# A ring of weight parts: two places of 1024 columns become four of 512, made and given back by halves

## The chip, the cores and the metric

The kernel runs on one core of a Trainium2 chip. The metric is the device time of one launch in microseconds. A core has TensorE (matrix products; PE in the rows, its weight loads PEld), VectorE (DVE), ScalarE (ACT), GpSimd (POOL) and SyncE (SP, whose queue issues most of the transfers here). Each engine works through its own instructions in order and meets the others at semaphores.

## What is computed

Two model blocks over one sequence of 512 tokens of width 1024, all in float32. The first block mixes tokens in three ways (RWKV-7, S5, gated linear attention), merges them by gates, adds a cross attention to 256 memory tokens and a feed-forward layer with a short convolution. The second has an attention layer with a context of 256 tokens, an HGRN2 layer and a gated feed-forward layer after each. Nearly all of the arithmetic is in products of the tokens with weight matrices:

```
p_rw, p_s5, p_gla, p_gate = _split(h @ w_in[l], IN_SIZES)
gates = jax.nn.sigmoid(p_gate).reshape(B, L, N_BRANCH, D_MODEL)
merged = (gates[:, :, 0] * (y_rw @ w_branch[l, 0])
          + gates[:, :, 1] * (y_s5 @ w_branch[l, 1])
          + gates[:, :, 2] * (y_gla @ w_branch[l, 2]))
x = x + merged @ w_out[l]
x = x + cross_attention(rms_norm(x, norm_xattn[l]), mem_n, xa_wq[l], xa_wkv[l], xa_wo[l])
x = x + conv_ffn(rms_norm(x, norm_ffn[l]), ffn_w_up[l], ffn_conv[l], ffn_conv_b[l], ffn_w_down[l])
```

## The kernel before

Activations lie with features on the 128 partitions and tokens along the columns. To keep float32 accuracy at the matrix engine's faster rate, both operands of a product are split into a high part (a cast to float32r) and a low part (the value less its high part), and three products are summed: low weight by high token, high by low, high by high. The activations' parts (`hh`, `hl`, `mh`, `ml` and others) are made once; the weights' parts are made each time that a weight passes.

A weight, in this text, is what one call of `Stream.weights` (L194) handles: up to eight rows of 128x128 (`ks` rows, 1024 columns in all), or four rows of 256 columns for products whose result has the tokens on the partitions (`tokens`, L245). It passes through two rings. `raw` has three places of 1024 columns, which SyncE's queue fills from HBM (`load`, L189). `parts` has two places of 1024 columns for the high part and two for the low one (`Stream(b, 3, 2)`, L2230). ScalarE casts the whole weight into `wh` (L200), VectorE subtracts the whole into `wl` (L204). In some passages (`st.help` set) the rows are halved for the subtraction alone: VectorE takes the first half, GpSimd the second. Then `multiply` (L233) runs the rows in order on TensorE, three products for each row and each set of tokens (L240; L262 to L264 where weights are the moving operand, L1195 for gates made ahead). When the last of them is done, the place is free for the weight after next.

Most weights have eight rows. Those of `w_branch` and `w_glu` have four and use half a place. The last third of each feed-forward layer's second matrix has six rows, `hg_wo` is taken in calls of four and three rows and one call for its last rows (`last`, L2203). `first_products` (L1230) makes four weights at once in a pool of its own ("first").

Two things set the order of the work. The program is written with fillers: generators whose steps (products, for example) are dropped into chains of small dependent operations. And a scheduler of the framework then lists each engine's instructions by its own model of their times and by the order in the program, waiting for free places of the rings among them. So a change in the rings also moves instructions that it doesn't name. `closing` (L272) is the passage at the end of a layer: the last products run for one half of the tokens, then for the other, while the first half's norm runs beside them; `st.help` is set in it.

The places that the prediction names: the S5 layer (its chain on VectorE through L1052 to L1120, with the scan L1115) has the merge of the first mixer beside it (`merge`, L1203: a gate's weight of eight rows, then a branch's weight of four, then a step on VectorE, L1218, and for later mixers the gate read back from HBM, `th`); `conv_ffn` (L1318) is the first block's feed-forward layer, with the context's norm (`Context.steps`) as its filler.

Of the kernel before, what the change touches and what calls it, by code (L numbers as in the profile page):

```python
# [9 lines left out]
F32 = mybir.dt.float32  # L10
F32R = mybir.dt.float32r
# [6 lines left out]
P = 128  # L18
# [157 lines left out]
class Stream:  # L176
# [16 lines left out]

    def weights(self, src, ks, m=P, parts=None):  # L194

        nc = self.b.nc
        raw = self.load(src, ks, m)
        h, l = ((parts or self.parts).tile([P, 1024], F32R, tag=n, name="w" + n)[:, : ks * m]
                .rearrange("p (k m) -> p k m", m=m) for n in "hl")
        nc.scalar.copy(h, raw)  # L200
        c = ks - ks // 2 if self.help else ks
        for e, s in ((nc.vector, slice(0, c)), (nc.gpsimd, slice(c, ks))):
            if s.stop > s.start:
                e.tensor_tensor(l[:, s], raw[:, s], h[:, s].bitcast(F32), op=ALU.subtract)  # L204
        return h, l

    def accumulators(self, kinds):

# [23 lines left out]

    def multiply(self, parts, ks, sets):  # L233
        nc = self.b.nc
        h, l = parts
        for k in range(ks):
            s = sets(k)
            for w, x, n in ((l, 1, 0), (h, 2, 1), (h, 1, 2)):
                for z in s:
                    nc.tensor.matmul(z[0], w[:, k], z[x], start=k == 0 and n == 0, stop=k == ks - 1 and n == 2)  # L240

    def features(self, *a, **kw):
        for _ in self.products(*a, **kw):
# [2 lines left out]
    def tokens(self, W, ks, xs, ts, gs, take):  # L246


        nc = self.b.nc
        for i, g in enumerate(gs):  # L250
            parts = []
            for q in range(ks // 4):
                h, l = self.weights(W[g, q], 4, 256)
                parts += [(h[:, k], l[:, k]) for k in range(4)]
            for two in [[t] for t in ts[:-2]] + [ts[-2:]]:
                accs = [self.accumulator()[:, :256] for _ in two]
                for q in range(0, ks, 4):
                    for acc, t in zip(accs, two):
                        for k in range(q, q + 4):
                            xh, xl = (z[:, t * P : (t + 1) * P] for z in xs(k))  # L260
                            wh, wl = parts[k]
                            nc.tensor.matmul(acc, xh, wl, start=k == 0, stop=False)  # L262
                            nc.tensor.matmul(acc, xl, wh, start=False, stop=False)  # L263
                            nc.tensor.matmul(acc, xh, wh, start=False, stop=k == ks - 1)  # L264
                for acc, t in zip(accs, two):
                    take(i, t, acc)
                    yield
# [915 lines left out]
def gates(b, st, xs, ns, made, wk, ps):  # L1183


    nc = b.nc
    dram = b.pool("gates", 1, DRAM)
    for n in ns:
        for m in range(8):
            acc = ps.tile([P, 512], F32, tag="ps", name="gate")  # L1190
            h, l = st.weights(b.a["w_gate"][8 * n + m], 8)
            for k in range(8):
                xh, xl = xs(k)
                for w, x, i in ((l, xh, 0), (h, xl, 1), (h, xh, 2)):
                    nc.tensor.matmul(acc, w[:, k], x, start=k + i == 0, stop=k == 7 and i == 2)  # L1195
                if k < 7:
                    yield
            th = wk.tile([P, 512], F32, name="gate", tag="gate")
            nc.scalar.activation(th, acc, AF.Tanh, scale=0.5)
            made[n, m] = dram.tile([P, 512], F32, name=f"gate{n}{m}")  # L1200
            nc.scalar.dma_start(made[n, m], th)
            yield
# [26 lines left out]
def first_products(b, st, W, tiles, h, units, accs, late, side):  # L1229


    hh, hl = h
    with ExitStack() as c:
        pool = b.pool("first", len(tiles), ctx=c, side=side)
        st.help = True
        parts = {m: st.weights(W[m], 8, parts=pool) for m in tiles}
        st.help = False
        for n, (at, to) in enumerate(units):
            for i, m in enumerate(tiles):
                st.multiply(parts[m], 8, lambda k: [(accs[n][m][:, to], hh[:, k, at], hl[:, k, at])])  # L1240
                if n == 0 and i == 1:
                    late()
# [848 lines left out]
def block2(b, st, X, h, late, old_, c, out, ctx):  # L2091
# [86 lines left out]
    with ExitStack() as c1:  # L2178
# [25 lines left out]
        def products(p):  # L2204

            for i in range(8):
                acc = st.accumulator()[:, :256]
                st.multiply([z[:, i : i + 1] for z in last], 1, lambda k: [(acc, *(z[:, p.t] for z in o[7]))])
                add_gated(b, p.X, m.gt1)(i, acc)
                yield  # L2210

# [14 lines left out]
def body(tc, a, out):  # L2226
    with ExitStack() as ctx:
        b = Builder(tc, ctx, a)
        b.common()
        st = Stream(b, 3, 2)  # L2230
        mod = [b.cp.tile([P, 48, 2], F32, name=f"mod{l}") for l in range(2)]
        context = Context(b, ctx, mod)
        c = ctx.enter_context(ExitStack())
        block2(b, st, *block1(b, st, ctx, c, context), context, c, out, ctx)
# [16 lines left out]
```

## Time and profile before

| | us |
|---|---|
| median of three runs | 3227.83 |
| lowest and highest of them | 3222.96, 3229.99 |
| the profiled execution | 3222.53 |
| its span, from first to last instruction | 3220.2 |
| TensorE busy in the span | 3089.4 |
| VectorE, ScalarE, GpSimd busy | 1800.2, 1171.2, 781.7 |
| mean granted clock of TensorE | 0.98 of full speed |

How to read it: the engines work side by side, so the busy times don't add up; a matmul counts as busy up to a modelled end, and the next one starts before that end. The granted clock is the share of TensorE's full speed in a stretch.

### The profile page before, as it was taken

Reading aid. Unit: us, or ns where it says so; the run is one execution under the profiler, and the core shown is the slowest. Engines: PE = TensorE matmul, PEld = TensorE weight load, DVE = VectorE, ACT = ScalarE, POOL = GpSimd, SP = SyncE. Lnnn points to the kernel's source line nnn. Section 1 sums busy time; section 2 is a strip of 40 time slices with the busy share of each in tenths; the row PEclk is TensorE's granted clock in tenths of the full one; section 3 lists DMA queues with packets and bytes.
Section 4 is the critical chain, followed back from the end, with each engine's and each line's share of the span. In section 5 each row is a group of like instructions: output and inputs, shape, how many; then the busy total and the mean of one; then the engine's idle time right before and its main releaser. Section 6 shows DMA issues by size and latency. Waiting matters only on the chain.

```text
span 3220.2 us, 50507 instructions
## 1 busy us (share of the span) xinstructions
PE 3089.4 (96%) x20456; PEld 2644.9 (82%) x20456; DVE 1800.2 (56%) x3067; ACT 1171.2 (36%) x2009; POOL 781.7 (24%) x827
## 2 busy tenths in 40 slices
PE   7999889989999999999999999999999999899998
PEld 6888767769797878896669988888889998788887
DVE  6444475556565555777766684323555555753434
ACT  4233224324344333545654321212444444332223
POOL 3322131220040000568775000000323222310003
PEclk9999989999999999999999999999999999989999
DMA  3122123333245232432224473222321111123333
GB/s 132 57 73 80 38 75 97 98 117 124 78 133 188 89 95 89 134 107 72 80 84 144 146 243 129 61 64 62 109 91 53 53 51 49 53 76 95 98 98 112
DMA packets 114776, 308.11 MB, mean 96 GB/s; under 512 B 32224, under 2 KB 37040, under 8 KB 114032
## 3 DMA queue, kind: packets, MB, share of 16 engines
q1 hardware_dynamic: 109904, 293.94, 29.1%
q10 hardware_dynamic: 4640, 10.95, 0.9%
q8 instruction: 161, 2.64, 0.3%
q14 instruction: 71, 0.58, 0.1%
HBM read 295.18 MB, written 8.39 MB: 94 GB/s over the span
## 4 chain that ended last, share of the span: by engine, by line
PE 84%; DVE 7%; issue 2%; POOL 2%; DMA 2%; ACT 2%; DVEq 0%; POOLq 0%; SPq 0%; ACTq 0%
PE acc L240 57%; PE ps L524 3%; PE gate L1195 3%; PE acc L262 2%; DVE wl L204 2%; PE acc L263 2%; PE acc L264 2%; PE ps L1980 2%; PE mods L1490 1%; PE ss L346 1%; PE sc L1745 1%; PE st L1766 1%; DMA w<-in_ada_dram 1%; DVE y L435 1%; PE acc L1788 1%
## 5 line engine op out<-in xcount | busy, mean ns | idle before, releaser
L240 PE MATMUL acc<-hh,wl 128*128 128x512 f32 (+1 forms) x2296 | 762.3, 364 | 12.3 <-DVE wl L204 7.0
L240 PE MATMUL acc<-hh,wh 128*128 128x512 f32 (+1 forms) x2296 | 759.7, 362 | 0.0
L240 PE MATMUL acc<-hl,wh 128*128 128x512 f32 (+1 forms) x2296 | 758.6, 362 | 0.0
L200 ACT CAST wh<-raw 128x1024 fp32r<-128x1024 f32 (+3 forms) x472 | 460.2, 977 | 580.6 <-PE acc L240 427.0
L204 DVE TENSOR_TENSOR wl<-raw,wh 128x1024 fp32r<-128x1024 f32 (+2 forms) x472 | 527.4, 1118 | 221.5 <-ACT wh L200 214.3
L204 POOL TENSOR_TENSOR wl<-raw,wh 128x512 fp32r<-128x512 f32 (+1 forms) x120 | 169.2, 1413 | 1299.6 <-ACT wh L200 756.1
L240 PEld LDWEIGHTS acc<-hh,wl 128*128 128x128 f32 x2296 | 403.1, 189 | 88.9 <-DVE wl L204 9.4
L240 PEld LDWEIGHTS acc<-hh,wh 128*128 128x128 f32 x2296 | 403.0, 189 | 68.7 <-issue 1.8
L240 PEld LDWEIGHTS acc<-hl,wh 128*128 128x128 f32 x2296 | 402.6, 189 | 65.3 <-issue 0.5
L240 PE MATMUL acc<-mh,wl 128*128 128x512 f32 (+1 forms) x848 | 266.5, 340 | 14.3 <-DVE wl L204 14.1
L240 PE MATMUL acc<-ml,wh 128*128 128x512 f32 (+1 forms) x848 | 261.4, 333 | 0.2 <-DVE ml L340 0.2
L240 PE MATMUL acc<-mh,wh 128*128 128x512 f32 (+1 forms) x848 | 261.3, 333 | 0.0
L240 PEld LDWEIGHTS acc<-mh,wl 128*128 128x128 f32 x848 | 151.6, 189 | 36.1 <-DVE wl L204 18.3
L240 PEld LDWEIGHTS acc<-ml,wh 128*128 128x128 f32 x848 | 152.1, 189 | 17.5 <-DVE ml L340 0.4
L240 PEld LDWEIGHTS acc<-mh,wh 128*128 128x128 f32 x848 | 151.8, 189 | 17.4
L1604 ACT ACTIVATE t<-acc 128x512 f32<-128x512 f32 x66 | 34.7, 527 | 343.6 <-PE acc L240 343.5
L1556 DVE SCALAR_TENSOR_TENSOR X<-acc,mod,X 128x256 f32<-128x256 f32 (+1 forms) x112 | 65.4, 593 | 160.6 <-PE acc L240 160.6
L1605 DVE SCALAR_TENSOR_TENSOR t<-t,acc 128x512 f32<-128x512 f32 x66 | 39.4, 596 | 161.9 <-ACT t L1604 161.9
L262 PE MATMUL acc<-wl,hh 128*128 128x256 f32 x448 | 126.8, 285 | 1.8 <-DVE wl L204 1.0
L263 PE MATMUL acc<-wh,hl 128*128 128x256 f32 x448 | 127.0, 284 | 0.0
L264 PE MATMUL acc<-wh,hh 128*128 128x256 f32 x448 | 126.9, 285 | 0.0
L1606 DVE TENSOR_TENSOR t<-t,acc 128x512 f32<-128x512 f32 x66 | 39.4, 598 | 137.6 <-PE acc L240 137.1
(604 smaller groups left out, 5823.3 us busy)
## 6 DMA issues: line engine op xcount, KB each, us to landing
raw<-in_ffn_in_dram SPq DMA_DIRECT2D x88, 512.0 KB, 3.5
ada<-in_ada_dram SPq DMA_DIRECT2D x48, 512.0 KB, 3.9
w<-in_ada_dram SPq DMA_DIRECT2D x48, 512.0 KB, 4.5
raw<-in_ffn_w_up_dram SPq DMA_DIRECT2D x44, 512.0 KB, 3.5
raw<-in_ffn_out_dram SPq DMA_DIRECT2D x32, 512.0 KB, 3.5
raw<-in_hg_w_dram SPq DMA_DIRECT2D x32, 512.0 KB, 3.5
raw<-in_ffn_out_dram SPq DMA_DIRECT2D x40, 384.0 KB, 3.1
raw<-in_w_gate_dram SPq DMA_DIRECT2D x24, 512.0 KB, 3.6
```

The lines of the kernel that those rows point to most:

```text
L200: nc.scalar.copy(h, raw)
L204: e.tensor_tensor(l[:, s], raw[:, s], h[:, s].bitcast(F32), op=ALU.subtract)
L240: nc.tensor.matmul(z[0], w[:, k], z[x], start=k == 0 and n == 0, stop=k == ks - 1 and n == 2)
L262: nc.tensor.matmul(acc, xh, wl, start=k == 0, stop=False)
L263: nc.tensor.matmul(acc, xl, wh, start=False, stop=False)
L264: nc.tensor.matmul(acc, xh, wh, start=False, stop=k == ks - 1)
L524: nc.tensor.matmul(out(r, ci), lhsT(r, ci), rhs(r, ci), start=start, stop=stop)
L1195: nc.tensor.matmul(acc, w[:, k], x, start=k + i == 0, stop=k == 7 and i == 2)
L1556: return lambda i, acc: b.nc.vector.scalar_tensor_tensor(X[:, i], acc, gate[:, i : i + 1], X[:, i], op0=ALU.mult, op1=ALU.add)
L1605: nc.vector.scalar_tensor_tensor(t, t, 1.0, a, op0=ALU.add, op1=ALU.mult)
L1606: nc.vector.tensor_tensor(t, t, u, op=ALU.mult)
L1980: nc.tensor.matmul(p[:, c], kc[:, c * P : (c + 1) * P], qc[:, c * P : (c + 1) * P], start=True, stop=True)
```

## The change

`weights` makes parts of 512 columns. A weight of eight rows now takes two places in each ring of parts, one after the other: cast of the first four rows, subtraction, cast of the last four rows, subtraction. Four rows of 256 columns are cut into two times two rows. Where `st.help` is set, VectorE subtracts the first part and GpSimd the later one, so that six rows are now divided into four and two where they were three and three, and a weight of four rows of 128 is no longer divided. It returns a list of pairs of rows, and `multiply`, `tokens` and `gates` take the row's pair from it. The rings have four places of 512 columns instead of two of 1024 (`Stream(b, 3, 4)`), the pool "first" twice as many places of half the size: the memory is the same. `raw` and its transfers are as before.

```diff
     def weights(self, src, ks, m=P, parts=None):
 
+
         nc = self.b.nc
         raw = self.load(src, ks, m)
-        h, l = ((parts or self.parts).tile([P, 1024], F32R, tag=n, name="w" + n)[:, : ks * m]
-                .rearrange("p (k m) -> p k m", m=m) for n in "hl")
-        nc.scalar.copy(h, raw)
-        c = ks - ks // 2 if self.help else ks
-        for e, s in ((nc.vector, slice(0, c)), (nc.gpsimd, slice(c, ks))):
-            if s.stop > s.start:
-                e.tensor_tensor(l[:, s], raw[:, s], h[:, s].bitcast(F32), op=ALU.subtract)
-        return h, l
+        out = []
+        step = 512 // m
+        for n, k0 in enumerate(range(0, ks, step)):
+            c = min(step, ks - k0)
+            h, l = ((parts or self.parts).tile([P, 512], F32R, tag=t, name="w" + t)[:, : c * m]
+                    .rearrange("p (k m) -> p k m", m=m) for t in "hl")
+            x = raw[:, k0 : k0 + c]
+            nc.scalar.copy(h, x)
+            (nc.gpsimd if self.help and n else nc.vector).tensor_tensor(l, x, h.bitcast(F32), op=ALU.subtract)
+            out += [(h[:, k], l[:, k]) for k in range(c)]
+        return out
...
     def multiply(self, parts, ks, sets):
         nc = self.b.nc
-        h, l = parts
         for k in range(ks):
+            h, l = parts[k]
             s = sets(k)
             for w, x, n in ((l, 1, 0), (h, 2, 1), (h, 1, 2)):
                 for z in s:
-                    nc.tensor.matmul(z[0], w[:, k], z[x], start=k == 0 and n == 0, stop=k == ks - 1 and n == 2)
+                    nc.tensor.matmul(z[0], w, z[x], start=k == 0 and n == 0, stop=k == ks - 1 and n == 2)
...
             for q in range(ks // 4):
-                h, l = self.weights(W[g, q], 4, 256)
-                parts += [(h[:, k], l[:, k]) for k in range(4)]
+                parts += self.weights(W[g, q], 4, 256)
...
-        pool = b.pool("first", len(tiles), ctx=c, side=side)
+        pool = b.pool("first", 2 * len(tiles), ctx=c, side=side)
...
-                st.multiply([z[:, i : i + 1] for z in last], 1, lambda k: [(acc, *(z[:, p.t] for z in o[7]))])
+                st.multiply(last[i : i + 1], 1, lambda k: [(acc, *(z[:, p.t] for z in o[7]))])
...
-        st = Stream(b, 3, 2)
+        st = Stream(b, 3, 4)
```

`gates` is changed in the same way as `multiply`. The new lines move the line numbers: L200, L204, L1115, L1118, L1218 and L435 of the program before are L206, L207, L1118, L1121, L1222 and L438 of the changed one.

VectorE's order where the merge begins beside S5 (`ysl` is the low part of the first mixer's result, `M` the first merge step, `cs` and `tmp` belong to S5). Before, and then of the change:

```order
L1091 COPY m_4651<-mag_526 128x8x63
L340 SCALAR_TENSOR_TENSOR ysl<-Y_185,ysh 128x512 x3
L1218 SCALAR_TENSOR_TENSOR M<-th,acc 128x512
L204 TENSOR_TENSOR wl<-raw,wh 128x512
L1086 TENSOR_TENSOR tmp<-cs,ph 128x16
L1087 TENSOR_TENSOR tmp<-cs,ph 128x16
L204 TENSOR_TENSOR wl<-raw,wh 128x1024
```

```order
L1094 COPY m_4791<-mag_550 128x8x63
L343 SCALAR_TENSOR_TENSOR ysl<-Y_185,ysh 128x512 x3
L207 TENSOR_TENSOR wl<-raw,wh 128x512
L1222 SCALAR_TENSOR_TENSOR M<-th,acc 128x512
L207 TENSOR_TENSOR wl<-raw,wh 128x512 x2
L1089 TENSOR_TENSOR tmp<-cs,ph 128x16
```

Before, the first merge step, which waits for TensorE's sum, stood ahead of the next branch weight's subtraction of 512; now a subtraction of 512 stands ahead of that step, and two follow it.

VectorE's order further on in S5, from the scan (L1115, now L1118) to the next merge step (`E`, `R`, `sx`, `tmp` belong to S5). Before, and then of the change:

```order
L1115 SCALAR_TENSOR_TENSOR R<-m_4651,z 128x512
L1054 TENSOR_TENSOR E<-E,tmp 128x1024
L1091 COPY m_5138<-mag_526 128x8x63
L1065 TENSOR_TENSOR tmp<-pw,s5c 128x1152
L1118 TENSOR_TENSOR R<-R,cs 128x512
L204 TENSOR_TENSOR wl<-raw,wh 128x1024
L1218 SCALAR_TENSOR_TENSOR M<-th,acc 128x512
```

```order
L1118 SCALAR_TENSOR_TENSOR R<-m_4791,z 128x512
L207 TENSOR_TENSOR wl<-raw,wh 128x512
L1094 COPY m_5294<-mag_550 128x8x63
L1055 TENSOR_TENSOR E<-pw,bb 128x1024
L1121 TENSOR_TENSOR R<-R,cs 128x512
L1057 TENSOR_TENSOR E<-E,tmp 128x1024
L207 TENSOR_TENSOR wl<-raw,wh 128x512
L1123 TENSOR_TENSOR sx<-R,sw 128x8x64
L1068 TENSOR_TENSOR tmp<-pw,s5c 128x1152
L1222 SCALAR_TENSOR_TENSOR M<-th,acc 128x512
L207 TENSOR_TENSOR wl<-raw,wh 128x512 x2
```

The subtraction of 1024 stood behind the scan and four more S5 instructions; now one of 512 stands directly behind the scan, a second four instructions later, and two more behind the merge step.

VectorE's order at the end of the first block's feed-forward layer (`u`, `t` and `ml` belong to its last row of results; `y` and `hcl` to the context's norm). Before, and then of the change:

```order
L1337 SCALAR_TENSOR_TENSOR u<-acc,vt,u 128x511
L204 TENSOR_TENSOR wl<-raw,wh 128x384
L1338 SCALAR_TENSOR_TENSOR u<-acc,vt,u 128x510
L1356 TENSOR_TENSOR t<-t,u 128x512
L340 SCALAR_TENSOR_TENSOR ml<-t,mh 128x512
```

```order
L1341 SCALAR_TENSOR_TENSOR u<-acc,vt,u 128x511
L438 SCALAR_TENSOR_TENSOR y<-Xc,g_01_11830,rstd 128x256
L444 SCALAR_TENSOR_TENSOR hcl<-y,mod_70,hch 128x256
L1342 SCALAR_TENSOR_TENSOR u<-acc,vt,u 128x510
L207 TENSOR_TENSOR wl<-raw,wh 128x512
L438 SCALAR_TENSOR_TENSOR y<-Xc,g_01_11830,rstd 128x256
L444 SCALAR_TENSOR_TENSOR hcl<-y,mod_70,hch 128x256
L1360 TENSOR_TENSOR t<-t,u 128x512
L444 SCALAR_TENSOR_TENSOR hcl<-y,mod_70,hch 128x256
L343 SCALAR_TENSOR_TENSOR ml<-t,mh 128x512
```

The context's norm, which came some 150 rows earlier, now stands between the last steps. On TensorE, the first step of RWKV's first head pair (L559, now L562) stands in row 70 of its list where it stood in row 47.

## Rows read from the trace of the kernel before

**Rows 1.** The page, part 1: busy time, share of the span, instructions of each engine.

```profile
PE 3089.4 (96%) x20456; PEld 2644.9 (82%) x20456; DVE 1800.2 (56%) x3067; ACT 1171.2 (36%) x2009; POOL 781.7 (24%) x827
```

**Rows 2.** Table of stretches: busy us (instructions) by engine, granted clock, DMA share, GB/s.

```profile
400.00:720.00 320.00, 290.68 (x1490) 231.10 (x1489) 192.49 (x282) 111.04 (x182) 86.31 (x74) 0.95 0.31 95
1320.00:1345.00 25.00, 20.05 (x159) 19.57 (x158) 23.32 (x48) 16.31 (x33) 17.54 (x19) 0.89 0.61 182
2960.00:3040.00 80.00, 80.00 (x354) 66.12 (x353) 31.84 (x36) 21.22 (x27) 0.00 (x0) 1.00 0.30 96
```

**Rows 3.** List of waits of TensorE: us in total, times, longest us.

```profile
PE acc L240 <- DVE wl L204: 33.3, 34, 4.4
...
PE acc L262 <- DVE wl L204: 3.8, 5, 1.8
```

**Rows 4.** Timeline around 1099: start us, us, engine, line, operation, tiles, shapes.

```profile
1099.19 0.39 PE L240 MATMUL acc<-hh,wh 128*128 128x512 f32 x1
1099.42 0.39 PE L240 MATMUL acc<-hh,wl 128*128 128x512 f32 x1
...
1099.62 0.78 ACT L1336 ACTIVATE g<-acc,vt 128x512 f32<-128x512 f32 x1 [4.41 <-PE acc L240]
```

**Rows 5.** Groups by shape: busy us, mean ns | idle us before, what ended it.

```profile
L200 ACT CAST wh<-raw 128x1024 fp32r<-128x1024 f32 x371 | 387.4, 1046 | 475.2 <-PE acc L240 348.8 <-issue 49.7 <-POOL wl L204 28.4
...
L200 ACT CAST wh<-raw 128x768 fp32r<-128x768 f32 x56 | 46.3, 833 | 54.7 <-PE acc L240 29.9 <-POOL wl L204 16.2 <-issue 7.7
...
L200 ACT CAST wh<-raw 128x512 fp32r<-128x512 f32 x36 | 22.2, 616 | 39.9 <-PE acc L240 37.4 <-issue 1.3 <-PE acc L264 1.1
...
L204 DVE TENSOR_TENSOR wl<-raw,wh 128x1024 fp32r<-128x1024 f32 x307 | 389.1, 1268 | 170.6 <-ACT wh L200 169.3
```

**Rows 6.** Timeline, single subtractions on VectorE.

```profile
422.86 1.21 DVE L204 TENSOR_TENSOR wl<-raw,wh 128x1024 fp32r<-128x1024 f32 x1
...
426.64 0.68 DVE L204 TENSOR_TENSOR wl<-raw,wh 128x512 fp32r<-128x512 f32 x1
...
1301.60 0.56 DVE L204 TENSOR_TENSOR wl<-raw,wh 128x384 fp32r<-128x384 f32 x1 [0.15 <-ACT wh L200]
```

**Rows 7.** Timeline of TensorE at 422 and 702, and the chain at 694.

```profile
422.81 0.50 PE L240 MATMUL acc<-ysh,wl 128*128 128x512 f32 x1 [1.22 <-DVE wl L204]
...
702.37 0.50 PE L240 MATMUL acc<-ysh,wl 128*128 128x512 f32 x1 [2.13 <-DVE wl L204]
...
694.61 4.63 DMA th<-gate
```

**Rows 8.** Timeline at 438 and 466 to 470, and the chain at 470.

```profile
438.53 0.79 PE L240 MATMUL acc<-hh,wl 128*128 128x512 f32 x1 [2.33 <-DVE wl L204]
...
470.27 0.80 PE L240 MATMUL acc<-hh,wl 128*128 128x512 f32 x1 [4.37 <-DVE wl L204]
...
466.59 3.63 DVE L204 TENSOR_TENSOR wl<-raw,wh 128x1024 fp32r<-128x1024 f32 x1
...
466.08 3.06 POOL L1066 TENSOR_TENSOR Gm<-Gm,tmp 128x1152 f32<-128x1152 f32 x1
...
470.27 7.81 PE acc L240 x22
```

**Rows 9.** Timeline of TensorE at 499 and 1929.

```profile
499.15 0.50 PE L240 MATMUL acc<-hh,wl 128*128 128x512 f32 x1 [0.29 <-DVE wl L204]
...
1929.55 0.62 PE L240 MATMUL acc<-mh,wl 128*128 128x512 f32 x2 [1.40 <-DVE wl L204]
```

**Rows 10.** Timeline of TensorE at 926 and 3196, of ScalarE at 1300.

```profile
926.80 0.39 PE L240 MATMUL acc<-xqh,wl 128*128 128x256 f32 x1 [0.29 <-DVE wl L204]
...
3196.28 0.58 PE L240 MATMUL acc<-mh,wl 128*128 128x256 f32 x1 [2.45 <-DVE wl L204]
...
1300.74 1.56 ACT L200 CAST wh<-raw 128x768 fp32r<-128x768 f32 x2 [1.38 <-PE acc L240]
```

**Rows 11.** Groups by shape on VectorE, 400 to 720.

```profile
L204 DVE TENSOR_TENSOR wl<-raw,wh 128x1024 fp32r<-128x1024 f32 x22 | 35.0, 1589 | 27.5 <-ACT wh L200 27.5
```

More of the change, by code (lines that the diff above doesn't have):

```diff
@@ L1190, in gates @@
             acc = ps.tile([P, 512], F32, tag="ps", name="gate")
-            h, l = st.weights(b.a["w_gate"][8 * n + m], 8)
+            parts = st.weights(b.a["w_gate"][8 * n + m], 8)
             for k in range(8):
+                h, l = parts[k]
                 xh, xl = xs(k)
                 for w, x, i in ((l, xh, 0), (h, xl, 1), (h, xh, 2)):
-                    nc.tensor.matmul(acc, w[:, k], x, start=k + i == 0, stop=k == 7 and i == 2)
+                    nc.tensor.matmul(acc, w, x, start=k + i == 0, stop=k == 7 and i == 2)
                 if k < 7:
```

## The prediction

> **What bounds the kernel now.** Read the page's busy line first: TensorE is busy 96% of the span [rows 1], so only its idle time and a lower clock can be won back. The table of stretches says where they are [rows 2]. In the last feed-forward block (2960 to 3040) TensorE is busy 80.00 of 80 us at full clock: nothing that makes weights earlier helps there. Between 400 and 720 (the S5 and GLA mixers with the merge's products beside them) it is busy 290.68 of 320 at a granted clock of 0.95, and in a closing passage (1320 to 1345) 20.05 of 25, while VectorE is busy 23.32 of those 25. The list of waits puts 33.3 + 3.8 = 37.1 us of TensorE's idle time, in 39 waits, on the low part `wl` of a weight [rows 3]. These are what the change is about, 1.2% of the span.
>
> A weight that is made early is handed over without a charge of its own: ScalarE takes a finished sum at 1099.62; the last matmul before it started at 1099.19 and the first of the next weight at 1099.42, the same 0.23 us as inside a weight [rows 4]. So more hand-overs per weight cost TensorE nothing as long as they are early.
>
> **The change, term by term.** Sizes first. A cast of 1024 columns takes 1046 ns, of 768 833, of 512 616, and most of the idle time ahead of the large ones ends when TensorE gives a place back (348.8 of 475.2 us) [rows 5]. A subtraction on VectorE with no neighbour takes 1.21 us for 1024 columns, 0.68 for 512, 0.56 for 384 [rows 6]. So a weight of eight rows costs ScalarE 2 x 616 - 1046 = 186 ns more and VectorE 2 x 0.68 - 1.21 = 0.15 us more, but its first half is ready (1.046 - 0.616) + (1.21 - 0.68) = 0.96 us sooner, 0.53 of it if only the subtraction is late. TensorE then has 12 matmuls, 2.8 us at 512 columns and 1.4 if 256 take half as long, before it asks for the second half, which is ready about 0.7 us after the first. So where the halves are made one after the other, no second half is waited for.
>
> *Term 1, weights of four rows* (w_branch, w_glu: 128x512, which had a whole place of 1024 until now). They are not cut; four instead of two are now in flight. Six waits, 0.34 to 2.13 us, sum 6.63 [rows 7] (the first and the last). At the first of them the new order of VectorE puts the subtraction ahead of the merge step that waits for TensorE. I take the three outside the last merge as gone (2.34) and half of the other three (4.29), since there the gate's transfer, 4.63 us on the chain [rows 7], comes next: 4.5. Bounds 0 and 6.6.
>
> *Term 2, weights of eight rows subtracted by VectorE alone.* Twelve waits, sum 13.82. Two stand out, 2.33 and 4.37 us, in S5 [rows 8]. There the subtraction sits behind scan, products and copies in VectorE's queue, and at 466.59 it takes 3.63 us because GpSimd works from 466.08 for 3.06 us [rows 8]. In the new order three subtractions of 512 stand between two merge steps where one of 512 and one of 1024 stood, and the nearest to the scan comes directly ahead of it at the earlier place and directly behind it at the later; which weight it makes the order doesn't say, by the count a gate's first half. I take both waits as gone: 6.7. The other ten run from 0.24 to 2.04 us [rows 9] (the first and the last): each shrinks by 0.96 where the subtraction waited for its cast (0.96, 0.24 and 2.04 give 0.96 + 0.24 + 0.96), by 0.53 where it stood behind other VectorE work (0.29, four that sum to 1.38, 0.81 and 1.40 give 0.29 + 1.38 + 0.53 + 0.53): 4.9. Term 2 is 11.6; bounds 0 and 13.8.
>
> *Term 3, weights shared with GpSimd* (closings, first products, the context's projection). Sixteen waits, 0.28 to 2.45 us, sum 14.7 [rows 10] (the first and the last). VectorE's piece keeps its size (eight rows) or grows from 384 to 512 columns (six rows, +0.12 us); the cast before it is 0.43 or 0.22 shorter, and the place comes free 12 or 6 matmuls of 256 columns, 1.4 or 0.7 us, earlier, which matters where the cast waited for TensorE (1.38 us at 1300.74 [rows 10]). The six-row firsts (1.33, 1.33, 1.32, 2.45) gain about 0.8 each, two of 1.63 and 1.83 about 1.1 each, the ten small ones a part of their 4.8; I take 6.5 in all. Bounds 0 and 14.7.
>
> *Term 4, the clock.* After the 4.37 us wait 22 matmuls take 7.81 us instead of 22 x 0.23 = 5.06 [rows 8]; the engine had been idle for 4.37 us, and the granted clock of the whole stretch is 0.95, a mixture of its two levels [rows 2]. I count 2 of these 2.75 us back. Bounds 0 and 2.75.
>
> *Term 5, what is added.* ScalarE gets 371 x 0.186 + 56 x about 0.2 = 80 us, VectorE 307 x 0.15 + 56 x 0.12 = 53 us [rows 5, 6]. Cover: ScalarE is busy 36% and VectorE 56% of the span [rows 1], and where TensorE is full it is free. On the path lie the cut weights of S5 and GLA: 22 of eight rows [rows 11] x 0.15 = 3.3, of which I take 1.5, since VectorE is idle there 127 of 320 us [rows 2]. Then the closings of six-row weights, four passages of about 12 us in which VectorE is as full as at 1320 to 1345; at 18 matmuls of 0.115 us a weight these hold some 22 weights, 22 x 0.12 = 2.6, taken as 3 with the second casts. The order also moves the context's norm to the end of the first block's feed-forward; five of its VectorE steps of 256 columns, 0.42 us each by the slope of the subtractions [rows 6], come ahead of the last `ml`: 1.5 of at most 2.1. Together 6. Bounds 0 and 3.3 + 7 + 2.1 + 5 = 17.4, where 7 is all 56 x 0.12 and 5 is the first head pair of RWKV, whose first step stands 23 matmuls of 0.23 us later in TensorE's order; I take nothing for it, since the products that pass it must be done anyway.
>
> The Trainium skill, Perfetto Trace Analysis, section Optimizing Scalar/DVE Operations, speaks against small instructions: each pays some 93 ns on ScalarE and 60 ns on VectorE, so grouping helps an engine that is full. The rows show more per cut, 186 and 150 ns [rows 5, 6]; by the page's figures, as an estimate, the 3.3 would be 1.3 and the sum under 1 us better.
>
> **Sum.** 4.5 + 11.6 + 6.5 + 2 - 6 = 18.6, say 19 us off. The profiled execution took 3222.53 us (span 3220.2 and 2.3 around it), 5.3 below the median of the three runs, 3227.83, and just under their lowest. So a profile of about 3203.5 and, against the median, **3209 us**, 0.6% faster.
>
> **Rivals.** *The waits move on* (no change, 3228 give or take 6). For: `wl` is often only the last of a row of late things; the gate's transfer, S5's chain on VectorE and the finished sums come next, and VectorE's queue is in order, so a half that waits for its place blocks what stands behind it. Then terms 1 to 4 give some 6 and term 5 takes them. Against: the two largest waits are met by an earlier place in the queue, and the clock returns with them.
>
> *Two turns at the door* (slower). VectorE's subtraction beside a GpSimd instruction takes 3.63 us instead of 1.21 [rows 6, 8]. Cut in two, it can run into GpSimd twice. In 400 to 720 GpSimd is busy 86.31 of 320 us, 27% [rows 2]; an instruction like that of 3.06 us [rows 8] leaves 1.5 on average, so 22 more subtractions lose 22 x 0.27 x 1.5 = 9. If that and all of the added work lie on the path and nothing is won, 17.4 + 9 = 26 us more: 3254. It decides from the point where VectorE has no idle time left in these stretches; it has 40% in 400 to 720, and 7% in the closing passage [rows 2]. The Trainium skill, SBUF — State Buffer, section SBUF: two separate sides, has such a VectorE instruction with two SBUF inputs and a GpSimd one shut each other out for a whole instruction. The 3.63 us agree: they end 1.1 us after GpSimd does.
>
> *All of it* (faster still): all of the 37.1 us and the clock, 39.9, with the added work hidden: 3188. Against: waits of 2 us that have other causes next in line.
>
> That the change doesn't do what it says is no case: the order shows 427 more casts and 307 more subtractions on VectorE, and none of more than 512 columns.
>
> **Chances.** Forecast (7 to 33 us off) 0.58; all of it 0.10; waits move on 0.18; two turns 0.14. A measurement of this kernel tells about 0.2%, 6.5 us, from no change. Faster 0.68, same 0.18, slower 0.14. The range, 3192 to 3238, leaves out most of the case of all and the worse half of the slower one; the likeliest case alone spans 3195 to 3221.
>
> **What would show it.** In the new profile: `wl` on TensorE's list of waits falls from 37.1 us to some 14; the two S5 waits are gone and the granted clock of that stretch rises above 0.95; casts of 512 take about 616 ns, subtractions 0.68 us; the last feed-forward block stays full. Wrong, if TensorE's list names another VectorE or ScalarE result for the same microseconds, if `wl` subtractions of 512 columns average well above 0.9 us, or if time comes from stretches in which no weight was waited for.

## The result and the profile after

The changed kernel takes 3180.1 us (median; 3174.7 to 3182.9), the kernel before 3228.9 on the same chip: a ratio of 0.9849 [0.9832, 0.9865], 49 us off. Run again later on another chip it gave 3186.1 against 3222.2, 0.9879 [0.9861, 0.9897], 36 us by the medians (3175 to 3185 had been expected of that run). The mean of the two ratios, 0.9864, some 44 us of 3225, is what the experiments below are compared with; the change was not run again beside most of them, so a difference of some 5 us to it tells nothing. The forecast was 3209, its range 3192 to 3238: right in sign, far too small, and the range missed.

The busy line and the span of the page of after:

```profile
span 3177.7 us, 51604 instructions
...
PE 3069.4 (97%) x20456; PEld 2634.9 (83%) x20456; DVE 1841.9 (58%) x3374; ACT 1246.9 (39%) x2436; POOL 748.0 (24%) x827
```

Against [rows 1] ScalarE has 76 us more work and VectorE 42, as Term 5 said (80 and 53). TensorE's idle time fell from 3220.2 - 3089.4 = 130.8 us to 108.3; the other 20 us came off its busy time, which holds what is too short to be listed as a wait, and the clock.

TensorE's list of waits, after (us in total, times, longest):

```profile
PE acc L244 <- DVE th L1222: 9.5, 6, 4.2
...
PE acc L244 <- DVE wl L207: 3.1, 5, 0.9
...
PE acc L265 <- DVE wl L207: 1.4, 3, 0.8
```

The waits for `wl` went from 37.1 us [rows 3] to 4.5; I had said 14. What is new at the top is `th`, the gate's buffer after the merge step. Between 400 and 720, where S5, GLA and the merges run, the list had before

```profile
PE acc L240 <- DVE wl L204: 13.6, 9, 4.4
PE acc L240 <- DVE th L1218: 2.1, 1, 2.1
PE acc L262 <- DVE wl L204: 1.0, 1, 1.0
```

and has no `wl` after, but there

```profile
PE acc L244 <- DVE th L1222: 9.5, 6, 4.2
PE acc L244 <- ACT th L1219: 1.9, 1, 1.9
```

The table of stretches, after (the second row is the closing passage of [rows 2], which now lies 27 us earlier):

```profile
400.00:720.00 320.00, 297.02 (x1514) 239.69 (x1513) 201.81 (x305) 115.84 (x207) 86.45 (x74) 0.95 0.32 96
1293.00:1318.00 25.00, 23.30 (x191) 23.01 (x189) 18.27 (x40) 18.12 (x41) 14.13 (x16) 0.94 0.60 180
```

In the closing TensorE is busy 23.30 of 25 us instead of 20.05. In S5 and GLA the granted clock is 0.95 as before (0.91 in the second profile of the same kernel).

The parts by shape, ScalarE's casts and VectorE's subtractions, after:

```profile
L206 ACT CAST wh<-raw 128x512 fp32r<-128x512 f32 x834 | 511.6, 618 | 812.9 <-PE acc L244 653.0 <-issue 68.6 <-PE gate L1199 28.2
```

```profile
L207 DVE TENSOR_TENSOR wl<-raw,wh 128x512 fp32r<-128x512 f32 x770 | 572.5, 746 | 495.9 <-ACT wh L206 492.2 <-PE ps L527 1.4
```

The sizes are as forecast (616 ns and, with its neighbours, below 0.9 us). Look at the idle time behind the bar: the casts still wait for TensorE to give a place back, and VectorE now waits 492 us for casts where it waited 169 for those of 1024 columns. Both engines stand ready more often than before, and wait for a free place or for a cast.

**Where the 42.5 us of span came from.** The stretches hold different work before and after, because the order is sorted anew. So I counted along the work done: the steps between the starts of neighbouring matmuls, each against the usual step of its width (230 ns at 512 columns, 118 at 256, the like for other shapes), and of those over 30 ns above it the excess, summed. The first column of numbers is the work done, in us. The sum falls by 40.4 us.

```
piece of the work                      before  after  after, second profile
0-320     RWKV                          76.2    67.8    65.9
320-640   S5, GLA, merges               93.6    90.4    99.4
640-1120  cross attention, convolution  36.3    26.4    26.7
1120-1200 its closing, qkv              21.3    16.6    18.0
1200-1440 attention                     43.7    43.1    43.6
1440-1520 attention's closing           17.6    10.8    12.4
1520-2080 first feed-forward, closing   14.5     8.3     8.5
2080-2800 HGRN, second feed-forward     42.1    47.0    45.8
2800-     last closing                   9.8     4.4     4.4
sum                                    355.3   314.9   324.7
```

Three of the terms of the forecast, 4.5 + 6.7 + 2 us, lay in S5, GLA and the merges, and nothing came there that two profiles of one kernel agree on. The 36 us outside came from RWKV, for which the forecast had nothing, and from cross attention, the closings and the feed-forward, for which it had the rest. Ahead of 400 the kernel before has no wait for `wl` in its list, so the 8 us of RWKV are one of the prediction's own signs of being wrong: time from a stretch in which no weight was waited for.

### The profile page after: what moved, and what is told of

Same layout as the page of the kernel before. It is cut to its first block, busy times and chain, and to the rows that moved or that the text cites. A ratio compares the mean times of both kernels' runs of the same rounds, so it can differ in the third digit from the quotient of the medians.

```text
span 3177.7 us, 51604 instructions
## 1 busy us (share of the span) xinstructions
PE 3069.4 (97%) x20456; PEld 2634.9 (83%) x20456; DVE 1841.9 (58%) x3374; ACT 1246.9 (39%) x2436; POOL 748.0 (24%) x827
## 4 chain that ended last, share of the span: by engine, by line
PE 88%; DVE 6%; POOL 2%; ACT 2%; issue 1%; DMA 1%; SPq 0%; DVEq 0%; POOLq 0%; ACTq 0%
PE acc L244 61%; PE ps L527 3%; PE gate L1199 3%; PE acc L265 2%; PE acc L266 2%; PE acc L267 2%; PE ps L1984 2%; DVE wl L207 1%; PE mods L1494 1%; PE ss L349 1%; PE rstd L425 1%; PE sc L1749 1%; PE st L1770 1%; PE pp L527 1%; PE acc L1792 1%
## 5 line engine op out<-in xcount | busy, mean ns | idle before, releaser
L207 DVE TENSOR_TENSOR wl<-raw,wh 128x512 fp32r<-128x512 f32 (+1 forms) x779 | 577.5, 744 | 495.9 <-ACT wh L206 492.2
L206 ACT CAST wh<-raw 128x512 fp32r<-128x512 f32 (+1 forms) x899 | 537.5, 603 | 829.8 <-PE acc L244 667.6
L207 POOL TENSOR_TENSOR wl<-raw,wh 128x512 fp32r<-128x512 f32 (+1 forms) x120 | 142.3, 1189 | 1096.5 <-ACT wh L206 1093.3
L354 POOL TENSOR_TENSOR rs<-rs,ct_all 128x2 f32<-128x2 f32 (+1 forms) x32 | 27.7, 866 | 448.1 <-DVE rs L416 448.1
L1780 POOL TENSOR_TENSOR pl<-pr,ph 128x512 fp32r<-128x512 f32 x75 | 103.0, 1383 | 9.0 <-ACT ph L1777 4.4
```

The lines of the kernel that those rows point to most:

```text
L206: nc.scalar.copy(h, x)
L207: (nc.gpsimd if self.help and n else nc.vector).tensor_tensor(l, x, h.bitcast(F32), op=ALU.subtract)
L1780: (nc.vector if n % 3 == 1 else nc.gpsimd).tensor_tensor(pl, pr, ph.bitcast(F32), op=ALU.subtract)
```

## Experiments

Theory A, the forecast's: a weight's first half is ready 0.96 us sooner because it is made by halves. Theory B: a place given back at half a weight lets the next cast start earlier (the lead). Theory C: four weights of four rows in flight instead of two. Theory D: the order that the queues get when everything is sorted anew. Ratios are to the kernel before, run on the same chip.

**1. Halves made, places whole.** Kernel before, with the halves as slices of one tile of 1024:

```diff
-        nc.scalar.copy(h, raw)
...
+        step = 512 // m
+        for n, k0 in enumerate(range(0, ks, step)):
+            s = slice(k0, min(k0 + step, ks))
+            nc.scalar.copy(h[:, s], raw[:, s])
+            (nc.gpsimd if self.help and n else nc.vector).tensor_tensor(l[:, s], raw[:, s], h[:, s].bitcast(F32), op=ALU.subtract)
```

> Halves are cast and subtracted one after the other, as in the change, but into one whole place of 1024 columns that is taken and given back whole (two such places, as before). If the gain comes from making the first half early, this run has nearly all of it: 35 to 45 us below the kernel before, TensorE's waits for wl at 5 to 12 us. If it comes from the ring (places taken and given back by halves, four weights of four rows in flight), this run is within 10 us of the kernel before, waits for wl still above 25 us. If the order that is sorted anew on TensorE's queue matters, the 8 us at the head of RWKV come or go with the place of the first RWKV matmul and not with wl.

Measured 3220.4, ratio 0.9992 [0.9978, 1.0006]. Its waits for `wl`:

```profile
PE acc L240 <- DVE wl L204: 28.4, 27, 3.5
```

With the 1.9 us of L262 that is 30.3 where it was 37.1: the waits shrank by some 7 us, and the time by 2.6 by the ratio, which its interval doesn't tell from nothing. Theory A, on which Terms 2 and 3 were worked out, is not the 44 us.

**2 and 3. The same for the shared weights alone, and for the others alone** (the loop under `if self.help:`, under `if not self.help:`, else the code of before).

> Kernel before; halves are made one after the other, in whole places, only for the weights that VectorE shares with GpSimd (closings, first products, the context's projection). Alone this is Term 3 without the ring: the prediction put it at 6.5 us off, at most 14.7. If Term 3 was mis-sized by its waits, 10 to 15 us off; if the places decide there (the cast waits for TensorE to give a place back), under 4 us.

> Kernel before; halves are made one after the other, in whole places, only for the weights that VectorE subtracts alone. Term 2 without the ring: the prediction put it at 11.6 us off, at most 13.8 in listed waits. If waits shorter than the list shows come back too, 15 to 30 us off; if the ring is needed for it, under 8 us. The sum of this run's gain and that of the shared weights alone, taken from the gain of halves for all of them, tells whether the two add up.

Shared alone: 3230.8, 1.0018 [1.0004, 1.0031], slightly slower. The others alone: 3221.1, 0.9980 [0.9967, 0.9993], 6.5 us off. So the cut is no gain for the shared weights, where Term 3 had its 6.5, and a small one for the others, where Term 2 had 11.6.

**4. Quarters.** The change with eight places of 256 columns:

```diff
-        step = 512 // m
+        step = max(256 // m, 1)
...
-        st = Stream(b, 3, 4)
+        st = Stream(b, 3, 8)
```

> The change once more: eight places of 256 columns, a weight made, taken and given back by quarters (GpSimd still takes the second half of the shared ones). It doubles what Term 5 prices: some 1,250 casts and as many subtractions more, at 0.186 and 0.15 us a cut some 150 us on ScalarE and 120 us on VectorE. If those costs lie on the path in S5, GLA and the closings, this is 5 to 20 us slower than the change; if they are hidden, it is within 6 us of it, or up to 10 us faster if what is left of the waits (about 5 us for wl) and the short ones still shrink.

Measured 3176.6, 0.9852 [0.9833, 0.9871]: not told from the change. The parts by shape, ScalarE and VectorE:

```profile
L206 ACT CAST wh<-raw 128x256 fp32r<-128x256 f32 x1732 | 680.9, 404 | 948.6 <-PE acc L244 825.4 <-PE gate L1199 44.4 <-PE acc L267 30.7
```

```profile
L207 DVE TENSOR_TENSOR wl<-raw,wh 128x256 fp32r<-128x256 f32 x1548 | 700.5, 462 | 624.7 <-ACT wh L206 617.8 <-POOL wl L207 1.3
```

Against the halves that is 128 us more on VectorE (700.5 - 572.5) and 143 us more on ScalarE (680.9 - 538.2, its three shapes together), and none of it shows in the time (on the two pages, where all of an engine's work counts, VectorE's busy time is 88 us more and ScalarE's 132). Nor does a finer ring win anything that shows.

**5. First row last.** The change, but the matmuls of a weight's first row are put at its end, so that the first half's place comes back only there. Casts, subtractions, matmuls and places are the same in number.

```diff
-        for k in range(ks):
+        for j, k in enumerate([*range(1, ks), 0]):
...
-                    nc.tensor.matmul(z[0], w, z[x], start=k == 0 and n == 0, stop=k == ks - 1 and n == 2)
+                    nc.tensor.matmul(z[0], w, z[x], start=j == 0 and n == 0, stop=j == ks - 1 and n == 2)
```

> The change, but each weight's rows are multiplied in the order 1, 2, ..., 0: the matmuls of its first row come last, so that both its places come back only at the weight's end. The same casts, subtractions, matmuls and places; four-row weights still hold one place each. Theory of the lead (a half place given back at the weight's middle lets the next cast start half a weight sooner): most of the gain goes, 25 to 45 us slower than the change, 3200 to 3225, and 20 us or more of waits for wl come back. Theory of the four-row weights (four instead of two in flight): the gain stays, within 8 us of the change. If only the new order of the queues made the gain, either may happen, but without wl in the list of waits.

Measured 3200.2, 0.9926 [0.9911, 0.9942]: of the 44 us some 20 are gone, less than the 25 to 45 that the lead was expected to take.

**6. The same for the shared weights alone** (`if self.help` picks the order).

> The same, but only for the weights that VectorE shares with GpSimd in the closings and the context's projection; all others give their places back by halves as in the change. Theory of the lead: what Term 3 is worth comes back alone; by the waits of the kernel before that is up to 14.7 us listed, and more if short waits hide beneath the modelled ends of the matmuls: 8 to 20 us slower than the change. Theory of the four-row weights: within 5 us of the change.

Measured 3197.7, 0.9917 [0.9901, 0.9933]: 17 us slower than the change, give or take 5, nearly as much as for all weights. The early return pays in the closings and the context's projection; what it pays elsewhere does not show in the difference of these two runs. Theory C has nothing to say to this run, in which the four-row weights are as in the change.

**7. Four rows, two places.**

```diff
-        step = 512 // m
+        step = 2 if ks * m == 512 else 512 // m
```

> The change, but a weight of four rows of 128 columns is made in two parts of two rows, each in a place of its own of 512 columns (half of it empty): such a weight holds two places again, so two of them are in flight as in the kernel before. Theory of the four-row weights: 5 to 15 us slower than the change, lost between 400 and 720. Term 1 as predicted: 4.5 us slower. Theory of the lead alone: within 5 us, since the parts still come back one after the other.

Measured 3181.2, 0.9864 [0.9849, 0.9880]: no loss. Theory C falls, and with it Term 1. (The same for `w_glu` and `w_branch` alone:

> The change, with the four-row weights of w_glu and w_branch alone (not those of the closings) in two parts of two rows. In the run that did so everywhere the stretch up to the merge's end came 9 us earlier than in the change, and the closings lost as much again. If both are effects of the parts, this run is 6 to 10 us faster than the change, some 3171; if the 9 us were a shift of work past the mark, it is within 3 us of it.

Measured 3182.9, 0.9873 [0.9850, 0.9895]: no 6 to 10 us came, so the 9 us in one profile are taken for a shift of work past the mark.)

**8. Three buffers for the gate** (`wm = b.pool("mgw", 3, ctx=mx)`).

> The change with three buffers instead of two for the gate tile th of the merge. In the change TensorE's waits for th (9.5 us in 6 waits) stand where those for wl stood in 400 to 720, and that stretch came out level. If those waits are the transfer of the gate that cannot start before its buffer is free, 4 to 10 us faster than the change, below 3176. If th is late because the merge step itself is late on VectorE, within 4 us of the change.

Measured 3180.7, 0.9864 [0.9845, 0.9883]: nothing, though `th` fell from 9.5 to 5.9 us:

```profile
PE acc L244 <- DVE th L1222: 5.9, 2, 3.9
PE acc L244 <- DVE ysl L343: 3.6, 2, 2.1
```

The next late thing, `ysl`, stands in its place. That stretch is a row of late results, as the rival "the waits move on" had it.

**9. A third whole place, in the last feed-forward and closing of the kernel before.**

```diff
+        if parts is None and self.more is not None:
+            self.n += 1
+            parts = self.more if self.n % 3 == 0 else None
...
+        st.more = b.pool("more1", 1, ctx=c)
```

> The kernel before, with a third whole place of 1024 columns in the last feed-forward block and its closing alone (every third weight uses it). It makes the lead longer without making anything by halves. There, after 3140, the change came 5 us nearer to the end. Theory of the lead: about 5 us off the kernel before, the waits for wl after 3140 gone. Theory that the halves themselves matter: no difference.

3221.7, 1.0002 [0.9988, 1.0016]. TensorE's list of waits from 3140 on had 3.8 us for `wl`, the longest 2.45 [rows 10], before; with the third place all that is left is

```profile
PE rstd L426 <- POOL rs L355: 2.1, 2, 1.1
```

Counted as in the table above, the last closing fell from 9.8 to 4.8 us, close to the change's 4.4, with weights still made whole. That is theory B in one trace, without any half. In the time, 5 us of 3223 cannot be told from nothing.

**10 to 12. What is left when nothing comes back early.** Between run 5 (3200) and run 1 (3220) 20 us had to be explained, though neither seemed to give a place back early.

> The run with each weight's first row multiplied last (3200.2), and the same now also in the products that keep two weights of 256 columns for several token tiles (values and qkv projections, L257): there each weight's first row closes its four, so its places come back together. Between that run and the kernel with whole places (halves made, 3220.4) 20 us are unexplained. If the early return in these token products is their cause, this run is 8 to 20 us slower than 3200; if not, within 5 us of it.

> The same as the run before it, and weights of four rows hold two places each: now nothing is given back by halves anywhere and no more weights are in flight than in the kernel before, though the parts are still tiles of their own. If the ring's lead is the whole of the gain, this run comes to where whole places with halves made were, 3215 to 3225. If it stays near 3200, some 20 us of the change come from something else: the separate tiles of the halves, or the order of the queues that is sorted anew with them.

Measured 3197.6 (0.9923) and 3197.5 (0.9924 [0.9905, 0.9942]): both stay near 3198; of the second the lead, as I understood it then, asked for 3215 to 3225. And the kernel with whole places, its four-row weights now cut too:

> Halves made one after the other in whole places (3220.4 when run), and the four-row weights too are cut, into two parts of 256 columns, still in one whole place. It differs from the run with first rows last everywhere and four rows in two places (3197.5) only in that the parts are regions of one tile and not tiles of their own. If the uncut four-row weights held the run with whole places back (8.7 of its 28 us of waits for wl lie in 400 to 705), this one is at 3200 to 3210. If the separate tiles, with the order that follows from them, are the cause, it stays at 3215 to 3225.

3217.4, 0.9986 [0.9974, 0.9999]. The four-row weights are not it. Then I saw in the trace that "first row last" is no full hold: the next cast takes the second half's place, and that is free three matmuls before the weight's end.

**13 and 14. Both places back together.** The last row's matmuls alternate with those of the first row:

```diff
+        order = [(k, n) for k in range(ks) for n in range(3)]
+        if ks > 1:
+            order = order[3:-3] + [(k, n) for n in range(3) for k in (ks - 1, 0)]
```

> The change, with each weight's first row put off to its end and its matmuls alternating with those of the last row, in the products and the gates: the two places come back within one matmul (0.12 or 0.23 us) of each other, not three (0.35 or 0.69 us) as in the run with the first row last. Theory of the lead, down to one row of it: 3210 to 3222, within 12 us of the kernel before. Theory that separate tiles, or the order that is sorted anew with them, give those 20 us: 3195 to 3203.

> The same for the weights shared between VectorE and GpSimd alone. With the first row last these alone cost 12 to 17 us against the change (3197.7). Theory of the lead, down to one row: more than that, 3200 to 3212. Theory of the separate tiles: as there, 3193 to 3202.

All weights: 3205.4, 0.9946 [0.9928, 0.9964]. Shared alone: 3203.2, 0.9938 [0.9923, 0.9954], 24 us slower than the change. The first came between the two ranges expected, the second in that of the lead. The place that the next cast takes comes back one matmul before the weight's end, where it came three before it: two matmuls of lead, 0.23 us in the closings, seem worth 7 us in each pair of runs (0.9923 to 0.9946, 0.9917 to 0.9938), but in neither pair do the intervals part. The list of waits of the first:

```profile
PE acc L246 <- DVE wl L207: 13.2, 20, 1.8
```

In a closing of the second, where each weight of six rows takes 2.04 us, ScalarE's casts show the lead directly:

```profile
1297.86 0.93 ACT L206 CAST wh<-raw 128x512 fp32r<-128x512 f32 x2 [0.79 <-PE acc L246]
1299.90 0.93 ACT L206 CAST wh<-raw 128x512 fp32r<-128x512 f32 x2 [0.79 <-PE acc L246]
```

A cast every 2.04 us, each released by TensorE: the first starts 0.35 us after the start of the last matmul that reads the place of the second half (1297.51, the last but one of its weight), and what it makes is wanted at 1300.14. The kernel before does the same with one cast of 768 columns:

```profile
1306.81 0.84 ACT L200 CAST wh<-raw 128x768 fp32r<-128x768 f32 x1 [0.97 <-PE acc L240]
1307.55 0.41 ACT L371 ACTIVATE sq<-X 128x256 f32<-128x256 f32 x1
1308.93 0.83 ACT L200 CAST wh<-raw 128x768 fp32r<-128x768 f32 x1 [0.97 <-PE acc L240]
```

The place comes back with the matmul of 1306.44; the weight is wanted at 1308.68, and VectorE's piece of it is ready at 1308.23. There is 0.45 us to spare, hardly more than one square of the norm in ScalarE's queue (0.41).

**15. Fillers ahead of RWKV's first matmul**, in the kernel before (`if hp == 0: b.fill(8)`):

> The kernel before with up to eight filler products ahead of RWKV's first matmul, so that this one comes later on TensorE's queue, as it does in the change: no weight is made otherwise. The wait for twd there (4.8 us) should go. If the order alone is worth that, 4 to 8 us off the kernel before; if it is only moved to a later place, within 3 us of it.

3220.8, 0.9991 [0.9980, 1.0001], but its profile still shows the 4.8 us wait for `twd`; the edit did not do what it was for, and whether the gain at the head of RWKV is order alone stays open.

**All runs by one count.** For every part the trace gives the end of its subtraction on VectorE (GpSimd's, where that alone makes it) and the start of the first matmul that reads it. Late: less than 0.25 us between the two. In the kernels with whole places a weight counts once.

```
kernel                                  parts  late  ratio to before
before                                    472    68  1
halves made, places whole                 472    51  0.9992
the same, four rows cut                   472    46  0.9986
both places back together, all            899    36  0.9946
both together, shared weights alone       899    28  0.9938
first row last, all                       899    30  0.9926
first row last, shared weights alone      899    26  0.9917
four rows in two places                   935    21  0.9864
the change                                899    17  0.9849, 0.9879
quarters                                 1741     5  0.9852
```

Which matmul reads which part is told by their order alone. Matched a second way, which leaves unclear parts out, the late ones are 64 before, 35 and 40 with whole places, 13 to 25 with the places held and 13 in the change: the two ends of the column are firm, the order in its middle and the 5 of the quarters are not.

The delays of the first table tell more. Here each step counts against the median step of its own shape in the kernel before, which makes the figures smaller and leaves their differences as they were (40.8 us between the sums of before and after); one profile each, us:

```
kernel                                  RWKV  cross attention,  attention's  sum
                                              convolution       closing
before                                  64.2  37.7              25.4         298.7
halves made, places whole               61.0  44.1              22.9         297.2
the same, four rows cut                 60.5  39.1              22.9         295.3
both places back together, all          59.9  39.9              21.9         293.0
both together, shared weights alone     55.9  29.1              24.9         280.5
first row last, all                     54.5  33.1              22.8         271.5
first row last, shared weights alone    55.6  26.0              22.8         272.1
the change                              55.4  24.9              17.7         257.9
the change, second profile              53.6  25.2              19.3         267.9
```

With both places of every weight held to its end, 35 of the 41 us of delays are back in that profile, though the parts are still tiles of their own. Cross attention, in which the two profiles of the change differ by 0.3 us, shows it best: its delays are back at those of before when all weights are held (39.9), and mostly stay away when only the shared ones are (29.1). So by these profiles the lead pays outside the closings too.

## Why the forecast was wrong

*What bounds the kernel.* Right: TensorE's waits for `wl`, which fell by 32.6 of 37.1 us. Early hand-overs cost nothing that shows: 427 more casts, and in the quarters another 842, left the time no longer.

*Terms 2 and 3, the step that failed.* "each shrinks by 0.96 where the subtraction waited for its cast", and "by 0.53 where it stood behind other VectorE work". That prices the making of a half and leaves the place as it is. Run 1 is exactly this and gained 2.6 us, not told from nothing; run 2, its piece in Term 3, lost 0.2%, and run 3, its piece in Term 2, gained 6.5 us of 11.6. What pays is the return of the place: for the shared weights alone 17 to 24 us (runs 6 and 14) against 6.5 in Term 3, whose upper bound of 14.7 is exceeded too. (That sum was wrong as well: the sixteen waits make 15.7, the ten small ones 5.8 and not 4.8, and five of 0.18 us stand in no term.) I had the row: 348.8 of 475.2 us idle ahead of the casts ended by TensorE giving a place back [rows 5]. With two whole places the next cast starts when a weight ends and its subtraction must be done before the following weight ends: in that closing 2.24 us (1306.44 to 1308.68 above) for 1.79 us of hand-over, cast and subtraction (1306.44 to 1308.23). With four halves the first half's place comes back half a weight sooner, or a third of one where there are six rows. I used this in one clause of Term 3, the place that comes free 12 or 6 matmuls earlier, and priced only the waits listed then, not the weights that came just in time (68 late weights by the count above, 39 waits in the list). The bound was none, since it counts only waits long enough to be listed.

*Term 1.* 4.5 us: not seen (run 7).

*The S5 part of Term 2, 6.7, and Term 4, 2 us.* Between 400 and 720 the waits for `wl` fell from 14.6 us to none listed, and those for `th` rose from 2.1 to 11.4: the rival "the waits move on" is what happened there, and the clock came out at 0.95 and 0.91. These 8.7 us and most of Term 1 were counted where nothing was to be had.

*Term 5.* 6 us: nothing. Run 4 doubles the cost and shows no loss. The cover named for it holds; nothing shows that it fails in the tight stretches. The Trainium skill's Perfetto Trace Analysis, section Optimizing Scalar/DVE Operations, says beside its fixed cost of each instruction that on engines that aren't full, breaking instructions up may complete work sooner where they hold up others. By run 1 (0.9992) the breaking up alone did not do it here; with places given back by pieces it did.

*Two turns at the door* did not come: subtractions of 512 on VectorE average 746 ns, little above the 0.68 of a single one.

*What stays open.* Parts that are tiles of their own, with both places held to nearly the end, gain 17 us (run 13); the same halves as slices of whole tiles gain 3 to 5 (runs 1 and 12), hardly told from none. The two matmuls of lead between runs 10 and 13 are another matter and do not explain these. The late parts (36 against 46 to 51) go with it, and so does a new order of all queues; I could not separate the two. The delays of run 13's profile hardly differ from those with whole places (293.0 against 295.3 and 297.2), but that profile is the slowest of its six executions, 3214.7 us where their median is 3205.4, so it need not hold the 17 us. RWKV, with 1 late weight of 35 before, lost 8 to 10 us of its delays. Some 4 of them go also with whole places: run 1's profile no longer lists the 4.8 us wait for `twd`, but one of 3.5 us for `wl` at that point. The others come back when all weights are held (59.9); why, with so few late weights, is not settled.

No run beat the change by more than its interval; quarters and four rows in two places can't be told from it.

## What to carry to other kernels

For a ring of buffers, ask first what the maker waits for. If its idle time ends with the consumer giving a place back, the quantity to work out is the lead, from a place's return to the moment its next content is wanted, against the time to make it; finer places raise the lead without more memory. Making the first piece sooner without that gave from nothing to 6.5 us here, of 44. Price the change from the slack of all hand-overs, the ones just in time included, and not from the listed waits, which are neither the sum nor a bound. In a stretch where several results are late one behind the other, book nothing until the last of them is priced.

## What was not expected of the hardware

One program, profiled twice, gave spans of 3177.7 and 3191.2 us, and S5's stretch differed by 9 us between them (90.4 and 99.4 in the table) with a granted clock of 0.95 and 0.91: a single profile can't tell 9 us there.

Matmuls of 256 columns follow each other at two paces: 118 ns in the closing of the kernel before (1304.44 to 1306.44, 17 steps) and 113 in that of after (1283.50 to 1285.54, 18 steps), with no wait in either. Both paces occur in every profile (median 118, lowest tenth 113 to 116), so the pace in one passage is no sign of a faster kernel.
